# Attention scores over 160 key columns in column order, slipped between long products, and probabilities of two heads transposed together

## The chip, the cores and the metric

One core of a Trainium2 chip runs the whole kernel. The time is the device time of one execution in microseconds (us); lower is better. The engines in the profile are PE (TensorE, matrix products), PEld (TensorE loading the stationary operand of a product), DVE (VectorE), ACT (ScalarE), POOL (GpSimd) and SP (SyncE, which issues most transfers).

## The reference

An encoder of two layers on 256 tokens of width 1024. The tokens are a grid of 4 rows by 64 columns.

```
for l in range(DEPTH):                                   # 2
    x = x + 0.5 * swiglu(rms_norm(x), gate, up, down)    # width 2816
    z = rms_norm(x) @ w_in                               # 1024 -> 4352
    qa, ka, va, qs, ks, vs, zg = split(z)
    o_na = neighbourhood_attention(norm(qa), norm(ka), va, rpb)      # 8 heads of 64
    o_sw = sliding_window_gqa(norm(qs), norm(ks), vs, t5_bias, sink) # 8 heads, 2 kv heads
    g = sigmoid(zg + b_gate)
    x = x + (g_A * (o_na @ P_A) + g_B * (o_sw @ P_B)) @ w_out
    x = x + 0.5 * swiglu(rms_norm(x), gate2, up2, down2)
```

In the neighbourhood attention a query at grid column c sees all 4 rows of a window of 16 columns around c, clamped at the borders, with a bias per head from a table of relative rows and columns. All other scores are masked. In the sliding-window attention a query sees the keys up to 128 tokens away, with a bias by relative position (the same for both layers) and a sink term in the sum. Token s stands at row s // 64 and column s % 64.

## The kernel before

The 256 tokens are two tiles (t = 0, 1) of 128 partitions. All products are made in three parts: each operand is split into a high part and the rest (`wh` by ScalarE, `wl` by VectorE, in `split_to`, lines 184 and 185), and `three` (lines 170 to 172) adds xh wh, xh wl and xl wh into one PSUM bank. Such a product has 512 columns and is called a long product here.

TensorE's order is written by hand: Python emits its instructions in the order in which the chip runs them. `tick` advances a counter `now` by one for each three long products, and what was put aside with `defer(lag, ...)` is emitted when the counter reaches its time; `need` emits it earlier. The order on the other engines is made by a scheduler, which prefers what stands under `high_priority` (`urgent` below).

A layer is ffn, mix, ffn. `mix` makes its projections in the order of the string `ORDER` (Q, K: sliding-window queries and keys; q, k, v: those of the grid; g: gates; aN: the next of the 16 heads comes due N ticks later), so attention runs between the long products of the projections. `attend` handles a head in three steps:

- `front`: four score products (two token tiles, high and low part of the keys, line 568) into a bank of the tag "sc" (two buffers); VectorE adds the bias and takes the maximum (line 571), ScalarE the exponentials with their sums (line 574) and for the sliding window the sink `es` (line 578), VectorE the reciprocal, GpSimd scales the probabilities `S` (line 581).
- `turn`, `P_LAG` = 10 ticks later: TensorE transposes the four 128 x 128 blocks of `S` into the bank "pt" (one buffer, line 589), and `split_to` makes `ph` and `pl`.
- `back`, `V_LAG` = 7.5 ticks later: four products with the values (line 603) into one half of the bank "po" (one buffer, one tile for two heads); ScalarE copies the one part of it (`o`, line 607), VectorE adds the other (line 608); after the odd head `o` is split into `oA` or `oB`.

`MORE` adds ticks to the lag of single heads. `gates` (lines 655, 656) is an addition on VectorE and a tanh on ScalarE. `relative` fills a vector of 511 biases per head on GpSimd (line 484, 18 pieces) and stores it in device memory (`vec_d`); `sw_bias` loads 128 shifted rows of it per head. `na_bias` loads a head's part of the table in two transfers and GpSimd adds the mask of the columns (line 675). `S` is one of `LAG` = 3 buffers.

Of the kernel before, what the change touches and what calls it, by code (L numbers as in the profile page):

```python
# [21 lines left out]
P = 128  # L22
# [14 lines left out]
HB = NRR * NRC  # L37
T2W = 5 * NRC + GW
# [20 lines left out]
def hybrid_encoder(ctx, tc, x, w_gu1, w_d1, w_in, b_gate, qk_gain, rpb, sink, t5,  # L59
# [36 lines left out]
    qkg = const.tile([P, L, 4], F32, name="qkg")  # L96
    mask = const.tile([P, GW], F32, name="mask")
    snk = const.tile([P, L * NH], F32, name="snk")
# [13 lines left out]

    pad(const, "pad_c", 416)
    blank = ring.tile([P, 2, 512], F32R, name="blank", tag="wl", bufs=RING)
# [49 lines left out]
    def tick(cost):  # L164
        now[0] += cost
        while later and later[0][0] <= now[0]:
            later.pop(0)[3]()

    def three(ps, xh, xl, wh, wl, first, last):
        nc.tensor.matmul(ps, xh, wh, start=first, stop=False)  # L170
        nc.tensor.matmul(ps, xh, wl, start=False, stop=False)  # L171
        nc.tensor.matmul(ps, xl, wh, start=False, stop=last)  # L172

# [297 lines left out]

    vec_d = dram.tile([NH, 511], F32, name="vec_d")

    def relative():
        vec = act.tile([P, 512], F32, name="vec", tag="xg", bufs=2)[:NH, :511]
        table = small.tile([NH, 32], F32, name="table", tag="table", bufs=1)
        with tc.issue_after(rstd_done[0].ins):
            nc.gpsimd.dma_start(vec, c_band)
            nc.gpsimd.dma_start(table, t5)
        for a, n, b, step in _runs(_t5_constants()[0]):  # L480
            src = table[:, b:b + 1].to_broadcast([NH, n]) if step == 0 else table[:, min(b, b + step * (n - 1)):][:, :n]
            if step < 0:
                src = flipped(src)
            nc.gpsimd.tensor_tensor(vec[:, a:a + n], vec[:, a:a + n], src, ALU.add)
        nc.gpsimd.dma_start(vec_d, vec)

    def mix(l, n, after):
        with tc.tile_pool(name="mix", bufs=1) as mp:
# [51 lines left out]

            def attend(name, ins, qT, kh, kl, kidx, bias_of, vcol, ready, oT, sink_l=None):
                oh, ol = oT
                po = [None, None]
                with tc.issue_after(rstd_done[0].ins):
                    bias = [bias_of(0), bias_of(1)]
# [8 lines left out]
                def front(h):  # L554
# [3 lines left out]
                    b = bias.pop(0)  # L558
                    least = FMAX
# [3 lines left out]
                    S_ = mp.tile([P, T, S], F32, name="S", tag="S", bufs=LAG)  # L563
                    mx = small.tile([P, T], F32, name="mx", tag="mx")
                    sm = small.tile([P, T], F32, name="sm", tag="sm")
                    for t in range(T):
                        for i, k in enumerate((kh, kl)):
                            nc.tensor.matmul(ps[:, t, :], qT[:, h, t * P:(t + 1) * P], k[:, kidx(h), :],  # L568
                                             start=i == 0, stop=i == 1)
                    for t in range(T):  # L570
                        nc.vector.tensor_tensor_reduce(S_[:, t, :], ps[:, t, :], b(t), -1.0, least,  # L571
                                                       ALU.add, ALU.min, mx[:, t:t + 1])
                    for t in range(T):
                        nc.scalar.activation(S_[:, t, :], S_[:, t, :], AF.Exp, bias=mx[:, t:t + 1], scale=-1.0,  # L574
                                             accum_out=sm[:, t:t + 1])
# [4 lines left out]
                    nc.vector.reciprocal(sm, sm)  # L580
                    nc.gpsimd.tensor_tensor(S_, S_, sm.unsqueeze(2).to_broadcast([P, T, S]), ALU.mult)  # L581
                    defer(P_LAG + MORE.get((name, h), 0), (name, h, 0), lambda: turn(h, S_))

                @urgent
                def turn(h, S_):
                    tp = ps_acc.tile([P, T, T, P], F32, name="pt", tag="pt")
                    for t in range(T):
                        for kt in range(T):
                            nc.tensor.transpose(tp[:, kt, t, :], S_[:, t, kt * P:(kt + 1) * P], ident)  # L589
                    ph = mp.tile([P, T, T, P], F32R, name="ph", tag="ph", bufs=2)  # L590
                    pl = mp.tile([P, T, T, P], F32R, name="pl", tag="pl", bufs=2)
                    split_to(ph, pl, tp)
                    defer(V_LAG, (name, h, 1), lambda: back(h, ph, pl))

# [63 lines left out]
            def sw_bias(h):  # L658
                b = mp.tile([P, 384], F32, name="t5b", tag="t5b", bufs=2)
                nc.sync.dma_start(b, bass.AP(tensor=vec_d.tensor, offset=vec_d.offset + h * 511, ap=[[1, P], [1, 384]]))  # L660
                return lambda t: b[:, P - t * P:P - t * P + S]

            def na_bias(h):
                t2 = mp.tile([P, T2W], F32, name="t2", tag="t2", bufs=2)
                for r in range(2):
                    nc.sync.dma_start(
                        t2[r * GW:(r + 1) * GW],
                        bass.AP(tensor=rpb.tensor,
                                offset=rpb.offset + (l * NH + h) * HB + (4 + r) * NRC + 15 - (GW - 1),
                                ap=[[1, GW], [1, T2W]]))  # L670
                b = mp.tile([P, T, ROWS, GW], F32, name="b", tag="b", bufs=2)
                base = t2[:, :]
                src = bass.AP(tensor=base.tensor, offset=base.offset + 2 * NRC,
                              ap=[base.ap[0], [-2 * NRC, T], [NRC, ROWS], [1, GW]])
                nc.gpsimd.tensor_tensor(b, src, mask[:, None, None, :].to_broadcast([P, T, ROWS, GW]), ALU.add)
                return lambda t: b[:, t].rearrange("p r c -> p (r c)")
# [3 lines left out]
            na = attend("na", ("q0", "q1", "k0", "k1"), qT, *kT, lambda h: h, na_bias,  # L680
                        lambda kt, h: va[:, kt, h, :], lambda: "v1" in done, oA)
            step = {
# [10 lines left out]
            for token in ORDER.split():  # L693
# [7 lines left out]
            need(*[("front", True, h) for h in range(NH)])  # L701

            def branch(br, acc, t, pieces, ks):
# [88 lines left out]
def _window_constant():  # L792
    q = np.arange(GW)[:, None]
    k = np.arange(GW)[None, :]
    start = np.clip(q - 8, 0, GW - 16)
    m = np.where((k >= start) & (k < start + 16), 0.0, NEG).astype(np.float32)
    return np.ascontiguousarray(np.concatenate([m, m], 0)[::-1])

# [46 lines left out]
```

## Time and profile before

| | |
|---|---|
| time, median of 3 runs | 1076.77 us (1076.62 to 1077.98) |
| profiled execution: time, span | 1076.94 us, 1075.2 us |
| granted clock of TensorE | 0.999 |
| busy: PE, DVE, ACT, POOL | 1068.2, 875.8, 671.5, 116.7 us |
| VectorE in line 185 (`wl` from `raw`) | 336 of 1219 ns each |
| ScalarE in line 184 (`wh` from `raw`) | 336 of 1045 ns each |
| transfers | 212.63 MB, 198 GB/s |

The span runs from the first to the last instruction of the execution, and the time contains some microseconds around it. In a row of the timeline stand the start in us, the duration in us, the engine, the line, the operation and what it writes and reads, with partitions x elements; "xN" joins N of them, and brackets hold the idle time before it and what ended it. In a row of the groups stand count, then busy time in us and mean ns of one, then the idle time before them and what released it.

### The profile page before, as it was taken

The page shows a single profiled execution, that of the slowest core. Times are in us where ns is not written, and L with a number is a line of the kernel's source. Part 1 is how long each engine was busy: PE and PEld are TensorE (multiplying, and loading weights), DVE is VectorE, ACT ScalarE, POOL GpSimd, SP SyncE. Part 2 cuts the span into 40 slices and gives each one's busy share as a digit, 9 for nine tenths or more (in the row PEclk, how much of TensorE's full clock was granted, in tenths as well). Part 3 has the DMA queues.
Part 4 walks back from the last instruction along what each step waited for, and adds up shares of the span by engine and source line. Part 5 has one row for each costly group of instructions (what it writes and reads, how often), then busy time and mean ns, then how long its engine had stood idle before and what let it go on. Part 6 is the DMA issues. An engine that isn't in the chain of part 4 may idle for free.

```text
span 1075.2 us, 14749 instructions
## 1 busy us (share of the span) xinstructions
PE 1068.2 (99%) x5125; PEld 890.3 (83%) x5125; DVE 875.8 (81%) x1337; ACT 671.5 (62%) x1014; POOL 116.7 (11%) x118
## 2 busy tenths in 40 slices
PE   8999999999999999999999999999999999999998
PEld 6888888888888888888888888888888888888887
DVE  6678799889886768869977887988898867778696
ACT  6566654788764556565565665557877646566552
POOL 1000120243520000000000000003534000000000
PEclk9999999999999999999999999999999999999999
DMA  7767656765654667756657765657666554776652
GB/s 247 227 214 237 215 190 191 228 194 155 192 188 137 198 199 246 242 168 191 214 162 238 227 213 185 199 153 247 177 195 185 176 175 160 237 231 203 188 196 89
DMA packets 98827, 212.63 MB, mean 198 GB/s; under 512 B 7568, under 2 KB 13744, under 8 KB 98752
## 3 DMA queue, kind: packets, MB, share of 16 engines
q1 hardware_dynamic: 98560, 211.60, 62.3%
q8 instruction: 40, 0.66, 0.2%
q14 instruction: 35, 0.29, 0.1%
q0 software_dynamic: 192, 0.08, 0.1%
HBM read 210.59 MB, written 1.06 MB: 197 GB/s over the span
## 4 chain that ended last, share of the span: by engine, by line
PE 97%; DMA 1%; ACT 1%; DVE 0%; issue 0%; SPq 0%; ACTq 0%
PE g L170 22%; PE g L172 22%; PE g L171 22%; PE acc L170 5%; PE acc L172 5%; PE acc L171 5%; PE tp L320 2%; PE sc L568 1%; PE po L603 1%; PE tp L170 1%; PE tp L171 1%; PE tp L172 1%; PE pt L589 1%; PE tp L201 1%; PE br L170 1%; PE br L171 1%
## 5 line engine op out<-in xcount | busy, mean ns | idle before, releaser
L185 DVE TENSOR_TENSOR wl<-raw,wh 128x1024 fp32r<-128x1024 f32 x336 | 405.7, 1219 | 65.5 <-ACT wh L184 61.8
L184 ACT ACTIVATE wh<-raw 128x1024 fp32r<-128x1024 f32 x336 | 346.7, 1045 | 117.3 <-DMA raw<-in_w_gu 51.4
L170 PE MATMUL g<-wh,xh 128*128 128x512 f32 (+1 forms) x976 | 383.1, 393 | 0.5 <-DVE hh L444 0.5
L172 PE MATMUL g<-wh,xl 128*128 128x512 f32 (+1 forms) x976 | 377.8, 387 | 0.0
L171 PE MATMUL g<-wl,xh 128*128 128x512 f32 (+1 forms) x976 | 377.5, 387 | 0.0
L172 PEld LDWEIGHTS g<-wh,xl 128*128 128x128 f32 x976 | 183.4, 188 | 39.1 <-DVE xl L185 1.5
L170 PEld LDWEIGHTS g<-wh,xh 128*128 128x128 f32 x976 | 183.6, 188 | 33.8 <-DVE hh L444 1.1
L171 PEld LDWEIGHTS g<-wl,xh 128*128 128x128 f32 x976 | 183.7, 188 | 33.4 <-DVE wl L185 0.6
L443 ACT ACTIVATE sg<-g,rs_y 128x256 f32<-128x256 f32 x88 | 41.1, 467 | 89.7 <-PE g L172 77.3
L444 DVE SCALAR_TENSOR_TENSOR hh<-g,rs_y,sg 128x256 f32<-128x256 f32 x88 | 42.3, 481 | 53.0 <-ACT sg L443 53.0
L170 PE MATMUL acc<-wh,hi 128*128 128x512 f32 x180 | 71.2, 395 | 0.0
L171 PE MATMUL acc<-wl,hi 128*128 128x512 f32 x180 | 70.2, 390 | 0.0
L172 PE MATMUL acc<-wh,lo 128*128 128x512 f32 x180 | 70.1, 390 | 0.0
L176 POOL TENSOR_TENSOR rs_y<-ms,mhalf 128x1 f32<-128x1 f32 x12 | 8.1, 678 | 556.5 <-DVE ms L222 548.0
L352 DVE TENSOR_TENSOR u<-raw 128x512 f32<-128x512 f32 x64 | 41.7, 686 | 20.9 <-DMA raw<-in_w_d 20.8
L184 ACT ACTIVATE corner<-raw 128x512 fp32r<-128x512 f32 x32 | 20.1, 629 | 40.4 <-DMA raw<-in_w_d 22.4
L581 POOL TENSOR_TENSOR S<-S,sm 128x512 f32<-128x512 f32 x32 | 37.2, 1161 | 65.6 <-DVE sm L580 38.3
L172 PEld LDWEIGHTS acc<-wh,lo 128*128 128x128 f32 x180 | 33.8, 188 | 7.2
L171 PEld LDWEIGHTS acc<-wl,hi 128*128 128x128 f32 x180 | 33.8, 188 | 6.7
L170 PEld LDWEIGHTS acc<-wh,hi 128*128 128x128 f32 x180 | 33.8, 188 | 6.7
L184 ACT ACTIVATE wh<-v 128x1024 fp32r<-128x1024 f32 x20 | 21.2, 1062 | 28.9 <-DVE v L352 24.5
L574 ACT ACTIVATE S<-S,mx 128x256 f32<-128x256 f32 x64 | 31.9, 499 | 8.0 <-DVE mx L571 7.9
(189 smaller groups left out, 1522.0 us busy)
## 6 DMA issues: line engine op xcount, KB each, us to landing
raw<-in_w_gu SPq DMA_DIRECT2D x176, 512.0 KB, 4.5
raw<-in_w_d SPq DMA_DIRECT2D x100, 512.0 KB, 4.2
raw<-in_w_in SPq DMA_DIRECT2D x64, 512.0 KB, 4.7
raw<-in_w_out SPq DMA_DIRECT2D x16, 512.0 KB, 3.6
bb<-in_b_gate SPq DMA_DIRECT2D x16, 256.0 KB, 3.6
raw<-in_w_bsw SPq DMA_DIRECT2D x8, 512.0 KB, 3.9
raw<-in_w_bna SPq DMA_DIRECT2D x8, 512.0 KB, 3.5
raw<-in_w_d SPq DMA_DIRECT2D x12, 256.0 KB, 2.7
```

The lines of the kernel that those rows point to most:

```text
L170: nc.tensor.matmul(ps, xh, wh, start=first, stop=False)
L171: nc.tensor.matmul(ps, xh, wl, start=False, stop=False)
L172: nc.tensor.matmul(ps, xl, wh, start=False, stop=last)
L184: linked("act", lambda: nc.scalar.activation(hi, src, AF.Copy))
L185: linked("dve", lambda: nc.vector.tensor_tensor(lo, src, hi.bitcast(F32), ALU.subtract))
L201: nc.tensor.transpose(tp[:, i, :], xs[t][:, k * P:(k + 1) * P], ident)
L320: nc.tensor.transpose(tp[:, SLOT[t][i], :], hh[:, t, i * P:(i + 1) * P], ident)
L352: sub = lambda to, x, y: nc.vector.tensor_tensor(to, x, y, ALU.subtract)
L443: linked("act", lambda: nc.scalar.activation(sg, ps[:, :FC], AF.Silu, scale=rstd[t]))
L444: linked("dve", lambda: nc.vector.scalar_tensor_tensor(pair[0][:, t], ps[:, FC:], rstd[t], sg, op0=ALU.mult, op1=ALU.mult))
L574: nc.scalar.activation(S_[:, t, :], S_[:, t, :], AF.Exp, bias=mx[:, t:t + 1], scale=-1.0, accum_out=sm[:, t:t + 1])
L581: nc.gpsimd.tensor_tensor(S_, S_, sm.unsqueeze(2).to_broadcast([P, T, S]), ALU.mult)
```

## The change

- The host permutes the tokens to column order (token = column * 4 + row) and the result back. A tile of 128 tokens is then 32 columns, and its windows lie in 40 columns: 160 keys instead of 256 (`NKEY`, `keys_of`). The grid scores, maxima, exponentials and scalings are 160 wide. The probabilities lie in five lasting tiles `R0` to `R4`, whose 96 other columns GpSimd clears at the start of each layer's mix.
- The first of a grid head's four scores is emitted in its place, the other three one by one behind the next long products, through the list `between` that `three` empties. The rest of `front` is `soften`, emitted with the last score.
- `turn` takes two heads, when the odd one is due. The first head's transposes go into a bank of the tag "po", the second's into "pt". `back` then runs for both heads, one directly after the other.
- `relative` stores four copies of the table, one for each grid row, each reordered by a ScalarE copy (`one`, 508 wide) and stored by a GpSimd transfer of its own. `na_bias` loads a head's table in one transfer instead of two and builds the bias in two halves.
- `LAG` is 5 instead of 3.

```diff
-LAG = 3
+LAG = 5
...
     def three(ps, xh, xl, wh, wl, first, last):
-        nc.tensor.matmul(ps, xh, wh, start=first, stop=False)
-        nc.tensor.matmul(ps, xh, wl, start=False, stop=False)
-        nc.tensor.matmul(ps, xl, wh, start=False, stop=last)
+        for x, w in ((xh, wh), (xh, wl), (xl, wh)):
+            nc.tensor.matmul(ps, x, w, start=first and x is xh and w is wh, stop=last and x is xl)
+            if between:
+                between.pop(0)()
...
-        nc.gpsimd.dma_start(vec_d, vec)
+        table_d = act.tile([P, 512], F32, name="one", tag="xg", bufs=2)
+        for r in range(ROWS):
+            one = table_d[32 * r:32 * r + NH, :DIAG * ROWS]
+            src = bass.AP(tensor=vec.tensor, offset=vec.offset + GW * r, ap=[vec.ap[0], [1, DIAG], [GW, ROWS]])
+            nc.scalar.activation(one.rearrange("p (u k) -> p u k", k=ROWS), src, AF.Copy)
+            nc.gpsimd.dma_start(vec_d[:, r, :], one)
...
+                    def score(t, i, k):
+                        nc.tensor.matmul(ps[:, t, :n], qT[:, h, t * P:(t + 1) * P], k[:, kidx(h), keys_of(t)],
+                                         start=i == 0, stop=i == 1)
+                    rest = lambda begun=now[0]: soften(h, b, ps, S_, mx, sm, least, sk, begun)
...
+                    if rows:
+                        scores[1:] = [urgent(fn) for fn in scores[1:]]
+                        scores[0]()
+                        while between:
+                            between.pop(0)()
+                        between.extend(scores[1:-1])
+                        between.append(lambda: (scores[-1](), rest()))
...
-                    defer(P_LAG + MORE.get((name, h), 0), (name, h, 0), lambda: turn(h, S_))
+                    held.append((h, S_))
+                    if h % 2:
+                        pair_, held[:] = list(held), []
+                        defer(P_LAG + MORE.get((name, h), 0) + begun - now[0], (name, h, 0), lambda: turn(pair_))
...
-                def turn(h, S_):
-                    tp = ps_acc.tile([P, T, T, P], F32, name="pt", tag="pt")
-                    for t in range(T):
-                        for kt in range(T):
-                            nc.tensor.transpose(tp[:, kt, t, :], S_[:, t, kt * P:(kt + 1) * P], ident)
...
-                    defer(V_LAG, (name, h, 1), lambda: back(h, ph, pl))
+                def turn(heads):
+                    tps = [ps_acc.tile([P, T, T, P], F32, name="pt", tag=tag) for tag in ("po", "pt")]
+                    for (_, S_), tp in zip(heads, tps):
+                        for t in range(T):
+                            for kt in range(T):
+                                nc.tensor.transpose(tp[:, kt, t, :], S_[:, t, kt * P:(kt + 1) * P], ident)
...
+                    defer(V_LAG, (name, heads[1][0], 1), lambda: [back(*r) for r in ready_])
...
+            rows = [mp.tile([P, T, S], F32, name=f"R{i}", tag=f"R{i}") for i in range(LAG)]
+            for r in rows:
+                nc.gpsimd.memset(r[:, 0, NKEY:], 0.0)
+                nc.gpsimd.memset(r[:, 1, :S - NKEY], 0.0)
...
-    x_in[:, HEAD:] = a["x"].reshape(S, D)
+    x_in[:, HEAD:] = a["x"].reshape(ROWS, GW, D).transpose(1, 0, 2).reshape(S, D)
```

How the rows of work move shows at three places. In these rows `g`, `po`, `pt` and `sc` are the bank written, and the rest names what is read.

TensorE before, first layer, sliding window: the last product of head 3 and then the transposes of head 5.

```order
L603 MATMUL po<-pl,sv 128x256
L170 MATMUL g<-wh,xh_1793 128x512
L171 MATMUL g<-wl,xh_1793 128x512
L172 MATMUL g<-wh,xl_1794 128x512
L170 MATMUL g<-wh,xh_1793 128x512
L171 MATMUL g<-wl,xh_1793 128x512
L172 MATMUL g<-wh,xl_1794 128x512
L589 MATMUL pt<-ident,S 128x128 x4
```

The bank "pt" of these transposes is not that of the products ahead of them. TensorE after, first layer, the last sliding-window turn (heads 6 and 7), behind the products of heads 4 and 5.

```order
L648 MATMUL po<-ph,sv 128x256
L648 MATMUL po<-pl,sv 128x256
L177 MATMUL g<-wh,xh_1745 128x512
L177 MATMUL g<-wl,xh_1745 128x512
L177 MATMUL g<-wh,xl_1746 128x512
L177 MATMUL g<-wh,xh_1745 128x512
L177 MATMUL g<-wl,xh_1745 128x512
L177 MATMUL g<-wh,xl_1746 128x512
L631 MATMUL pt<-ident,S 128x128 x8
```

The two rows of `po` end a group of eight, the same six long products follow, and the turn is one of eight transposes, the first four of them into the bank of `po`. Next TensorE before at a grid head's scores.

```order
L172 MATMUL g<-wh,xl_1794 128x512
L568 MATMUL sc<-kh,qT 128x256
L568 MATMUL sc<-kl,qT 128x256
L568 MATMUL sc<-kh,qT 128x256
L568 MATMUL sc<-kl,qT 128x256
L170 MATMUL g<-wh,xh_1793 128x512
```

The four scores stand together. TensorE after, at the first grid head.

```order
L587 MATMUL sc<-kh,qT 128x160
L177 MATMUL g<-wh,xh_1745 128x512
L587 MATMUL sc<-kl,qT 128x160
L177 MATMUL g<-wl,xh_1745 128x512
L587 MATMUL sc<-kh,qT 128x160
L177 MATMUL g<-wh,xl_1746 128x512
L587 MATMUL sc<-kl,qT 128x160
```

A long product stands between each two of them. Last VectorE before, at the products of the sliding-window heads 6 and 7 (`sm` is the sum of a head's exponentials).

```order
L185 TENSOR_TENSOR wl<-raw,wh 128x1024
L580 RECIPROCAL sm<-sm 128x2
L608 TENSOR_TENSOR o<-o,po 64x256
L185 TENSOR_TENSOR wl<-raw,wh 128x1024 x2
L185 TENSOR_TENSOR pl<-pt,ph 128x512
L608 TENSOR_TENSOR o<-o,po 64x256
```

Each head's addition `o` stands between other work. VectorE after, at the products of the sliding-window heads 2 and 3, behind which the turn of heads 4 and 5 comes.

```order
L705 SCALAR_TENSOR_TENSOR gate_1829<-g,rs_y,bb 128x512
L608 ISA S,mx<-sc,t5b,nsnk 128x256
L608 ISA mx 128x1
L608 ISA S,mx<-sc,t5b,nsnk 128x256
L608 ISA mx 128x1
L192 TENSOR_TENSOR wl<-raw,wh 128x1024
L616 TENSOR_TENSOR sm<-sm,es 128x2
L653 TENSOR_TENSOR o<-o,po 64x256
L617 RECIPROCAL sm<-sm 128x2
L653 TENSOR_TENSOR o<-o,po 64x256
```

The additions of both heads of a pair now stand one behind the other, behind a head's maxima (line 608) and a `wl`; the transposes of the next pair use their bank.

More of the change, by code (lines that the diff above doesn't have):

```diff
@@ L570, in front @@
-                    for t in range(T):
-                        nc.vector.tensor_tensor_reduce(S_[:, t, :], ps[:, t, :], b(t), -1.0, least,
+                    def score(t, i, k):
+                        nc.tensor.matmul(ps[:, t, :n], qT[:, h, t * P:(t + 1) * P], k[:, kidx(h), keys_of(t)],
+                                         start=i == 0, stop=i == 1)
+                    rest = lambda begun=now[0]: soften(h, b, ps, S_, mx, sm, least, sk, begun)
+                    scores = [lambda t=t, i=i, k=k: score(t, i, k) for t in range(T) for i, k in enumerate((kh, kl))]
@@ new lines, in front @@
+                    if rows:
[5 more added lines that the diff above has]
+                        between.append(lambda: (scores[-1](), rest()))
+                    else:
+                        for fn in scores:
+                            fn()
+                        rest()
+                @urgent
@@ L572, in front, with soften @@
+                def soften(h, b, ps, S_, mx, sm, least, sk, begun):
+                    live = [S_[:, t, keys_of(t)] for t in range(T)]
+                    for t in range(T):
+                        nc.vector.tensor_tensor_reduce(live[t], ps[:, t, :n], b(t), -1.0, least,
                                                        ALU.add, ALU.min, mx[:, t:t + 1])
                     for t in range(T):
-                        nc.scalar.activation(S_[:, t, :], S_[:, t, :], AF.Exp, bias=mx[:, t:t + 1], scale=-1.0,
+                        nc.scalar.activation(live[t], live[t], AF.Exp, bias=mx[:, t:t + 1], scale=-1.0,
@@ L680, in mix @@
             na = attend("na", ("q0", "q1", "k0", "k1"), qT, *kT, lambda h: h, na_bias,
-                        lambda kt, h: va[:, kt, h, :], lambda: "v1" in done, oA)
+                        lambda kt, h: va[:, kt, h, :], lambda: "v1" in done, oA, rows=rows)
             step = {
@@ L701, in mix @@
             need(*[("front", True, h) for h in range(NH)])
+            while between:
+                between.pop(0)()
             def branch(br, acc, t, pieces, ks):
```

73 lines of the change are left out of this document (41 added, 32 removed).

## Prediction

> **What bounds the kernel now.** I read the page first: busy shares, the clock by slices, the chain that ended last.
>
> ```profile
> span 1075.2 us, 14749 instructions
> PE 1068.2 (99%) x5125; PEld 890.3 (83%) x5125; DVE 875.8 (81%) x1337; ACT 671.5 (62%) x1014; POOL 116.7 (11%) x118
> PEclk9999999999999999999999999999999999999999
> PE 97%; DMA 1%; ACT 1%; DVE 0%; issue 0%; SPq 0%; ACTq 0%
> ```
>
> The chain is TensorE for 97% of the span, at full clock. The stretch that the change touches (224 to 330 us, the attention of one layer) was read by windows, for us, PE, PEld, DVE, ACT, POOL:
>
> ```profile
> 224.00:330.00 106.00, 106.00 (x580) 90.29 (x579) 92.00 (x193) 80.64 (x170) 37.84 (x29) 1.00 0.61 182
> ```
>
> TensorE has no idle time there, so whatever shortens or delays its row of work by 1 us moves the end by 1 us; other engines count only where TensorE waits for them. Next the timeline of TensorE around one turn (start, duration, line, operation). Durations overlap, since matmuls are pipelined; the price of one is the step from its start to the next start.
>
> ```profile
> 266.66 0.28 PE L603 MATMUL po<-ph,sv 128*128 128x256 f32 x1
> 266.77 0.28 PE L603 MATMUL po<-pl,sv 128*128 128x256 f32 x1
> ...
> 267.13 0.40 PE L170 MATMUL g<-wh,xh 128*128 128x512 f32 x1
> ...
> 268.30 0.39 PE L172 MATMUL g<-wh,xl 128*128 128x512 f32 x1
> 268.53 0.60 PE L589 MATMUL pt<-ident,S 128*128 128x128 f32 x4
> 268.88 0.48 PE L170 MATMUL g<-wh,xh 128*128 128x512 f32 x1
> 269.19 0.40 PE L171 MATMUL g<-wl,xh 128*128 128x512 f32 x1
> ...
> 269.66 0.28 PE L568 MATMUL sc<-kh,qT 128*128 128x256 f32 x1
> ...
> 270.02 0.28 PE L568 MATMUL sc<-kl,qT 128*128 128x256 f32 x1
> 270.14 0.40 PE L170 MATMUL g<-wh,xh 128*128 128x512 f32 x1
> 270.38 0.39 PE L171 MATMUL g<-wl,xh 128*128 128x512 f32 x1
> ```
>
> Prices: a long product (512 columns) 0.23 (six from 267.13 to 268.53 make 1.40); a 256-wide score or po product 0.12 (four from 269.66 to 270.14 make 0.48); the first long product behind such a group 0.24 (270.14 to 270.38).
>
> **The change part by part.** *Narrower scores.* 64 of TensorE's 5128 matmuls go from 256 to 160 columns, each now with a long product on both sides. No row has such a pattern. By width alone one would take 0.23 x 160/512 = 0.072. But each matmul also loads 128 columns of its own, and the nearest row for a matmul shorter than its successor's load is the end of a group of 128-wide transposes:
>
> ```profile
> 209.12 0.19 PEld L170 LDWEIGHTS g<-wh,xh 128*128 128x128 f32 x1
> 209.15 0.47 PE L170 MATMUL g<-wh,xh 128*128 128x512 f32 x1
> 209.23 0.19 PEld L171 LDWEIGHTS g<-wl,xh 128*128 128x128 f32 x1
> 209.46 0.40 PE L171 MATMUL g<-wl,xh 128*128 128x512 f32 x1
> ```
>
> The next load starts when the matmul ahead enters the array, and 209.12 to 209.23 is one load: 0.11. So a 160-wide score should cost 0.11, the load of the long product behind it, and not 0.072: 64 x (0.12 - 0.11) = 0.6 us gained; with the load hidden 64 x (0.12 - 0.072) = 3.1. I take 0.6, since 0.11 is read from a short matmul ahead of a long one, the same neighbours, and keep 3.1 as the end. The lower end is no gain.
>
> By the Trainium skill, page "TensorE: Matmul & The Clock Gate", section "LDWEIGHTS (loading the stationary operand)", a load takes about its columns over 1.2 ns, 107 ns for 128, whatever the contraction; that speaks against the narrowing, and the trace's 0.11 agrees. The same page's section "Back-to-back issue gap" gives N/2.4 + 2.5 ns, 69 ns for 160 columns, by which the gain would be 3.3 us; for 256 columns it gives 109 ns where this trace has 120, so the trace decides.
>
> *Four groups where one was.* Before, the four scores of a head stand together; after, each stands alone, so 48 more long products follow a short one. At 0.01 each (0.24 against 0.23) this is 0.5 us lost; ends 0 and 1.0. The 8 po products of two heads together make 16 fewer exits of that kind: -0.2.
>
> *Joined transposes.* Does a group of eight cost less than two of four? The nearest group of eight of the same width:
>
> ```profile
> 38.05 1.03 PE L320 MATMUL tp<-ident,hh 128*128 128x128 f32 x8
> 38.84 0.48 PE L170 MATMUL g<-wh,xh 128*128 128x512 f32 x1
> 39.16 0.39 PE L171 MATMUL g<-wl,xh 128*128 128x512 f32 x1
> ```
>
> Start to the second long product, less that one long product: eight cost 39.16 - 38.05 - 0.23 = 0.88, four 269.19 - 268.53 - 0.23 = 0.43. Twice four is 0.86: nothing gained.
>
> *The wait that comes with joining.* Before, every turn wrote bank "pt". Now the first head's four transposes write bank "po", which has one buffer and holds the products of the pair before until ScalarE's copy and VectorE's add (o) of both heads have read it. TensorE takes its row in order, so at that point it stops, with all long products queued behind it. How long after the first po product is a head's o done?
>
> ```profile
> 240.56 0.28 PE L603 MATMUL po<-ph,sv 128*128 128x256 f32 x1
> 241.23 0.38 ACT L607 ACTIVATE o<-po 64x256 f32<-64x256 f32 x1 [1.13 <-PE po L603]
> 241.64 0.41 DVE L608 TENSOR_TENSOR o<-o,po 64x256 f32<-64x256 f32 x1 [0.91 <-ACT o L607]
> ...
> 268.17 0.38 ACT L607 ACTIVATE o<-po 64x256 f32<-64x256 f32 x1
> ...
> 269.11 1.21 DVE L185 TENSOR_TENSOR wl<-raw,wh 128x1024 fp32r<-128x1024 f32 x1
> 270.25 0.41 DVE L608 TENSOR_TENSOR o<-o,po 64x256 f32<-64x256 f32 x1
> ```
>
> With both engines free, 242.05 - 240.56 = 1.49. The head whose products start at 266.66 needed 270.66 - 266.66 = 4.0: ScalarE finished a wh first, and VectorE a gate and two wl. For a pair the two o's alternate, ScalarE 0.38, VectorE 0.41 with 0.04 of hand-over each: 0.87 more, so 2.36 at best. By the written order TensorE reaches the turn after 8 po and six long products, 8 x 0.12 + 6 x 0.23 = 2.33, at three turns per layer: sliding-window heads 4 and 5, 6 and 7, and grid heads 6 and 7. Elsewhere 9 or 12 long products and up to four scores or eight transposes stand between (3.1 and more). The groups of the stretch give what is queued ahead of the o's (line, engine, operation, count | busy, mean ns | idle before):
>
> ```profile
> L185 DVE TENSOR_TENSOR wl<-raw,wh 128x1024 fp32r<-128x1024 f32 x30 | 38.0, 1273 | 6.4 <-ACT wh L184 6.4
> L184 ACT ACTIVATE wh<-raw 128x1024 fp32r<-128x1024 f32 x29 | 30.4, 1054 | 6.8 <-PE g L172 5.6 <-PE br L172 1.1
> L574 ACT ACTIVATE S<-S,mx 128x256 f32<-128x256 f32 x32 | 15.9, 499 | 4.0 <-DVE mx L571 4.0
> L655 DVE SCALAR_TENSOR_TENSOR gate<-g,rs_y,bb 128x512 f32<-128x512 f32 x8 | 5.9, 741 | 0.3 <-PE g L172 0.3
> L578 ACT ACTIVATE es<-mx,snk 128x2 f32<-128x2 f32 x8 | 2.3, 282 | 0.0
> ```
>
> Times from the moment at which TensorE wants the turn (first po at -2.33):
> - Heads 4, 5. ScalarE has first exp, wh, second exp, es ahead of its o's; wh becomes possible at -2.5 and ends at -1.46, the exp at -0.95, es at -0.67, the first copy at -0.29. VectorE's wl, which needs that wh, runs from -1.43 to -0.2, then sm, o to 0.35; copy to 0.77; second o to 1.2. Wait 1.2.
> - Heads 6, 7. The scores of the first grid head stand directly ahead of the po products; their reductions and exps run before and between the o's: the second o ends at 0.4. Wait 0.4.
> - Grid heads 6, 7. A gate (-2.84 to -2.1) and two wl, the second waiting for a wh that ends at -1.8, hold VectorE until 0.3; o, copy, o end at 1.5. Wait 1.5.
>
> The other turns end their walks 0.3 to 1.1 before TensorE comes. Both layers have the same order: 2 x (1.2 + 0.4 + 1.5) = 6.2 us. Ends: 0, if VectorE runs about a wl earlier than walked; and 2 x 3 x (4.0 + 0.87 - 2.33) = 15 if every tight turn is as late as the 4.0 above. I take the walk, since it orders the very rows. A wait lets both engines catch up, so the turn after it isn't late for it.
>
> *Table copies, queues.* Rows of ScalarE and GpSimd around the table:
>
> ```profile
> 140.41 0.60 ACT L184 ACTIVATE hi<-tp 128x512 fp32r<-128x512 f32 x1 [0.17 <-PE tp L320]
> 142.65 1.06 ACT L184 ACTIVATE wh<-v 128x1024 fp32r<-128x1024 f32 x1 [1.64 <-DVE v L352]
> 149.75 0.63 ACT L184 ACTIVATE corner<-raw 128x512 fp32r<-128x512 f32 x1 [2.68 <-DMA raw<-in_w_d]
> ...
> 132.09 9.24 POOL L484 TENSOR_TENSOR vec<-vec,table 8x165 f32<-8x165 f32 x18 [1.56 <-DMA vec<-in_c_band]
> 190.40 0.57 POOL L176 TENSOR_TENSOR rs_y<-ms,mhalf 128x1 f32<-128x1 f32 x1 [48.24 <-DVE ms L222]
> ```
>
> Four 508-wide copies stand behind hi, wait for the vector until 141.4 (132.09 + 9.24) and take about 0.55 each (hi, 512 wide, 0.60): until 143.6, so wh starts 1.0 late and ScalarE regains it in its 2.68 idle before 149.75. Nothing, with 1.0 as the upper end. GpSimd's three more table DMAs stand in its 48 us of idle; its 20 memsets and twice as many bias builds of half the work lie in its idle time (68 us of the 106 above); SP loses 16 DMAs. No turn waits longer for GpSimd's scaling by the order, since a pair's turn stands later behind its first head's scaling than before and its second head keeps its lag: nothing; if a pair's turn did wait, it would appear under rival two.
>
> The sum against the profiled execution (span 1075.2, 1.7 around it, 1076.9): -0.6 + 0.5 - 0.2 + 6.2 = +5.9, 1082.8. That execution is 0.2 above the median of the runs: 1082.7 forecast.
>
> **The rivals.** One: the waits as walked, but the load behind a score is hidden (0.072 a score): 2.4 us less, 1080.3. For it: in the rows of long products the loads are hidden; against it: 209.12 to 209.23. A reordering that pulls the load ahead, named by the Trainium skill, same page, section "LDWEIGHTS (loading the stationary operand)", would do this; here every load starts with or after the matmul before it.
>
> Two: more waits, each tight turn as late as the 4.0 of the row, 6 x 2.54 = 15, or two more turns per layer becoming late by about 1.3: 1088 to 1091. For it: the looser turns have as little as 0.3 in hand.
>
> Three, the other side: no wait. It decides at 2.33 against 2.36: where ScalarE and VectorE take the o's promptly, the bank is free as TensorE comes, and 1082.7 - 6.2 = 1076.5 is left, the same as before. For it: VectorE is 81% busy on the page, so it has spare time to run ahead of its queue; against it: in this stretch it is 92.0 of 106 busy, and one wl costs 1.27.
>
> Four: no wait and the load hidden: 1076.5 - 2.4 = 1074.1, faster.
>
> **How the numbers follow.** Forecast 0.56 (own range 1080.5 to 1085.5), rival one 0.15, two 0.08, three 0.13, four 0.08. The likeliest is 1082.7. The range takes in rival three and one and leaves out four and two: 1075.8 to 1087.4. A measurement tells about 0.2%, 2.2 us, from no change: faster is four less its tail above 1074.6 and rival three's below (0.08), same is three (0.14), slower the rest (0.78).
>
> **What the changed profile would show.** The scores: steps of 0.11 from each 160-wide score to the long product behind it (0.07 would prove rival one). The waits: idle time of TensorE ahead of the turns for heads 4 and 5, 6 and 7 of both kinds put down to VectorE's o, some 6 us in all, and TensorE's share of the chain lower by as much; without such rows rival three stands. ScalarE's copies: no idle of TensorE near 150. I would be wrong most of all if VectorE's queue stands ahead of where my walk puts it.

## The result

The changed kernel takes 1116.51 us (median of 4 runs, 1113.78 to 1118.25) against 1077.25 us (4 runs): 1.0362 times as long, interval 1.0349 to 1.0374. The forecast was 1082.7, with a range up to 1087.4. The direction was right and the size was not: 39 us were lost where 5.9 were forecast.

The page of the changed kernel, the same four lines as before:

```profile
span 1115.5 us, 14756 instructions
PE 1080.7 (97%) x5125; PEld 898.0 (81%) x5125; DVE 870.3 (78%) x1337; ACT 674.0 (60%) x1018; POOL 112.9 (10%) x157
PEclk9999999998999999999999999999999999999999
PE 81%; DVE 10%; ACT 3%; issue 3%; DMA 3%; POOL 0%; ACTq 0%; DVEq 0%; POOLq 0%
```

TensorE's share of the chain fell from 97% to 81%, VectorE's rose from 0 to 10%, and one slice of the clock is below full. The view of the waits names the place (us in total, times, longest):

```profile
PE po L648 <- DVE o L653: 27.8, 16, 2.3
```

TensorE does not wait at the turns. It waits inside the group of eight value products, once for each of the 16 pairs of heads. The timeline of TensorE at the first pair:

```profile
249.91 0.28 PE L648 MATMUL po<-ph,sv 128*128 128x256 f32 x1
...
250.26 0.28 PE L648 MATMUL po<-pl,sv 128*128 128x256 f32 x1
252.86 0.54 PE L648 MATMUL po<-ph,sv 128*128 128x256 f32 x1 [2.32 <-DVE o L653]
...
253.84 0.63 PE L177 MATMUL g<-wh,xh 128*128 128x512 f32 x1
254.26 0.63 PE L177 MATMUL g<-wl,xh 128*128 128x512 f32 x1
...
256.51 0.48 PE L177 MATMUL g<-wh,xh 128*128 128x512 f32 x1
256.83 0.40 PE L177 MATMUL g<-wl,xh 128*128 128x512 f32 x1
```

Four products of the first head run from 249.91. The second head's first product starts at 252.86, 2.60 after the product ahead of it, where 0.12 is its step: 2.48 lost. Over the 16 pairs these excess steps add up to 30.4 us (1.08 to 2.48 each). What ScalarE and VectorE did meanwhile:

```profile
249.92 1.21 DVE L192 TENSOR_TENSOR wl<-raw,wh 128x1024 fp32r<-128x1024 f32 x1
...
250.38 0.49 ACT L611 ACTIVATE S<-S,mx 128x256 f32<-128x256 f32 x1
...
250.88 0.49 ACT L611 ACTIVATE S<-S,mx 128x256 f32<-128x256 f32 x1
...
251.13 1.21 DVE L192 TENSOR_TENSOR wl<-raw,wh 128x1024 fp32r<-128x1024 f32 x1
...
251.67 0.38 ACT L652 ACTIVATE o<-po 64x256 f32<-64x256 f32 x1
...
252.40 0.40 DVE L653 TENSOR_TENSOR o<-o,po 64x256 f32<-64x256 f32 x1
```

Exponentials stand ahead of the first head's copy and two `wl` ahead of its addition, and as soon as that addition ends (252.80) the second head's products start (252.86). The two heads share one bank (one tile, `po`), and in this kernel a product waits until the other engines have done their reads of what was written there before it, although it writes the other half.

After the stop a long product takes 0.42 instead of 0.23 (253.84 to 254.26). Three windows of 3.41 us around it; behind the length stand the busy time of PE, PEld, DVE, ACT and POOL, then the granted clock, the busy share of the DMA engines and GB/s:

```profile
249.52:252.94 3.41, 1.10 (x8) 0.81 (x6) 3.36 (x11) 2.50 (x7) 0.37 (x1) 1.00 0.83 245
252.94:256.35 3.41, 3.41 (x13) 3.02 (x14) 1.33 (x3) 1.78 (x4) 1.67 (x2) 0.50 0.87 290
256.35:259.76 3.41, 3.41 (x23) 2.99 (x22) 2.94 (x5) 2.35 (x5) 0.00 (x0) 1.00 0.27 49
```

The clock is halved for exactly one such window, 1.7 us lost. There are five of them in the execution: 8.5 us. The rest of the loss lies far away, at 181 to 190 us, in three waits of 0.68, 1.00 and 0.35, 2.0 in all (below). 30.4 + 8.5 + 2.0 = 40.9 against a difference of spans of 40.3.

### The profile page after: what moved, and what is told of

It reads as the page before. It is cut to its first block, busy times and chain, and to the rows that moved or that the text cites. A ratio compares the mean times of both kernels' runs of the same rounds, so it can differ in the third digit from the quotient of the medians.

```text
span 1115.5 us, 14756 instructions
## 1 busy us (share of the span) xinstructions
PE 1080.7 (97%) x5125; PEld 898.0 (81%) x5125; DVE 870.3 (78%) x1337; ACT 674.0 (60%) x1018; POOL 112.9 (10%) x157
## 4 chain that ended last, share of the span: by engine, by line
PE 81%; DVE 10%; ACT 3%; issue 3%; DMA 3%; POOL 0%; ACTq 0%; DVEq 0%; POOLq 0%
PE g L177 58%; PE acc L177 10%; DVE wl L192 4%; DMA raw<-in_w_d 2%; PE br L177 2%; PE tp L177 2%; ACT wh L191 2%; PE tp L327 2%; PE po L648 1%; PE pt L631 1%; PE g L244 1%; PE tp L208 1%; PE sc L587 1%; DVE v L359 1%; DVE corner L192 1%
## 5 line engine op out<-in xcount | busy, mean ns | idle before, releaser
L177 PEld LDWEIGHTS g<-wl,xh 128*128 128x128 f32 x976 | 184.7, 189 | 34.6 <-DVE wl L192 0.6
L192 DVE TENSOR_TENSOR lo<-a,hi 128x896 fp32r<-128x896 f32 x32 | 33.8, 1086 | 0.6 <-ACT hi L191 0.6
L191 ACT ACTIVATE hi<-a 128x896 fp32r<-128x896 f32 x32 | 29.1, 942 | 7.9 <-DVE a L340 7.8
```

What stands on the lines that cost most here:

```text
L177: nc.tensor.matmul(ps, x, w, start=first and x is xh and w is wh, stop=last and x is xl)
L191: linked("act", lambda: nc.scalar.activation(hi, src, AF.Copy))
L192: linked("dve", lambda: nc.vector.tensor_tensor(lo, src, hi.bitcast(F32), ALU.subtract))
```

## The experiments

**Is it the joining?** `pairs_before` is the kernel before with only the joining (and five S buffers); `single` is the changed kernel with one head at a time. The main lines of the edit of `single` (`turn` and `back` then handle one head, as before):

```diff
-                    held.append((h, S_))
-                    if h % 2:
-                        pair_, held[:] = list(held), []
-                        defer(P_LAG + MORE.get((name, h), 0) + begun - now[0], (name, h, 0), lambda: turn(pair_))
+                    defer(P_LAG + MORE.get((name, h), 0) + begun - now[0], (name, h, 0), lambda: turn(h, S_))
...
```

> The kernel before with the joining alone: transposes of two heads together in the banks po and pt, the backs of both heads one after the other, five S buffers; old layout, four scores together, no table copies. Theory (bank): 16 stops of TensorE on VectorE's o, about 30 us, and 4 to 6 stretches of half clock, 7 to 10 us: 1112 to 1118. Rival (rest of the change): below 1095.

> The changed kernel with turn and back for one head at a time as before; column layout, 160-wide scores between long products, ScalarE's table copies and five S buffers stay. Theory (bank): the joining carries 38.9 of the loss, the table copies 2.0 and the scores 0: 1077.5 to 1080. Rival (rest of the change): layout, scores or copies carry a good part: 1085 or more.

Measured: `pairs_before` 1123.82 (ratio 1.0424, 1.0407 to 1.0442), `single` 1078.24 (1.0009, 1.0000 to 1.0018). The joining alone makes the whole loss and more, and `pairs_before` lies above its expected range of 1112 to 1118: its 16 stops come to 34.6 us by the steps, and nine windows, in eight stretches, have half clock. The view of its waits:

```profile
PE po L611 <- DVE o L616: 32.0, 16, 3.1
```

All the rest of the change costs about 1 us, the table copies below included.

**Is it the shared bank?** `banks` writes the second head's products into the other bank; `emit8` keeps one bank, but the program writes all eight products down ahead of the reads, so TensorE's row is the same word for word.

```diff
# banks
-                    if h % 2 == 0:
-                        po[0] = ps_acc.tile([P, 2, T, P], F32, name="po", tag="po")
+                    po[0] = ps_acc.tile([P, 2, T, P], F32, name="po", tag=("po", "pt")[h % 2])
# emit8, in back, now called once for both heads
+                    for h, ph, pl in heads:
+                        for kt in range(T):
+                            for i, p in enumerate((ph, pl)):
+                                nc.tensor.matmul(po[0][:, h % 2], vcol(kt, h), p[:, kt], start=kt + i == 0,
+                                                 stop=kt + i == 2)
+                    for h, ph, pl in heads:
...
+                        nc.scalar.activation(o[a:a + DH], ov[b:b + DH], AF.Copy)
+                        nc.vector.tensor_tensor(o[a:a + DH], o[a:a + DH], ov[a:a + DH], ALU.add)
```

> The changed kernel with the second head's value products in the bank of the tag pt, and the first head's in po. Theory (bank): no stop inside a pair, no half clock, 1116.5 - 38.9 = 1077.6; the second head's transposes come 0.4 us later than the first's, so the walked waits at the six tight turns come to about 4 us: 1078 to 1082. Rival (late engines): 1100 or more, with waits of the turns' transposes on VectorE's o.

> The changed kernel with one edit: all eight value products of a pair are written down ahead of the copy and the addition of both heads, so that TensorE's row stays the same and only its waits differ. Theory (bank): the second head's products stand in the bank that ScalarE and VectorE are reading for the first head, and TensorE stops 16 times, 30.4 us, which also brings 5 stretches of 3.4 us at half clock (8.5 us). Then both go, 38.9 us, and what may come is a wait at the three tight turns of a layer: my walk gave 6.2 us for the six, and reading starts 0.5 us later for each. Expected 1078 to 1087, best guess 1084. Rival (late engines): VectorE is behind whatever the bank, and the same wait only moves to the next turn: 1100 or more.

`banks` took 1082.98 (1.0055, 1.0040 to 1.0070), 0.98 above its expected interval; no stop in a pair, no half clock. What is left above `single` are waits at the three turns that the prediction had walked: 2.1 us per layer, 4.2 in all, one of them in the timeline of TensorE:

```profile
265.33 1.09 PE L631 MATMUL pt<-ident,S 128*128 128x128 f32 x8 [0.26 <-DVE o L653]
```

`emit8` took 1108.84 (1.0298, 1.0277 to 1.0320), and that is the rival's number. The stops left the pairs and came back at the turns, with three windows at half clock. Timeline of `emit8` at the first of them:

```profile
253.00 0.38 ACT L653 ACTIVATE o<-po 64x256 f32<-64x256 f32 x1
...
253.73 0.40 DVE L654 TENSOR_TENSOR o<-o,po 64x256 f32<-64x256 f32 x1
253.78 1.05 ACT L191 ACTIVATE wh<-raw 128x1024 fp32r<-128x1024 f32 x1
...
254.73 1.25 ACT L543 ACTIVATE kh<-tp,qkg 128x512 fp32r<-128x512 f32 x2
...
256.01 0.38 ACT L653 ACTIVATE o<-po 64x256 f32<-64x256 f32 x1
...
257.44 0.42 DVE L654 TENSOR_TENSOR o<-o,po 64x256 f32<-64x256 f32 x1
...
258.01 1.41 PE L631 MATMUL pt<-ident,S 128*128 128x128 f32 x8 [2.03 <-DVE o L654]
```

The second head's copy stands behind a short copy, a `wh` and two `kh`, 2.6 us after the first head's copy, and TensorE waits for the addition behind it. My reading: written first or not, copy, addition, copy, addition take turns in one bank, and the scheduler fills the pauses with long work. `emit8_copies_first` tests it and writes both copies ahead of both additions.

```diff
+                    for add in (False, True):
+                        for h, ph, pl in heads:
...
+                            if add:
+                                nc.vector.tensor_tensor(o[a:a + DH], o[a:a + DH], ov[a:a + DH], ALU.add)
+                            else:
+                                nc.scalar.activation(o[a:a + DH], ov[b:b + DH], AF.Copy)
```

> As emit8 (1108.84), and the two copies of a pair are written down ahead of the two additions. Theory (alternation): emit8 lost at the turns because copy, addition, copy, addition follow one another in one bank and the scheduler filled the second copy's waiting time with weights and keys, up to 3 us of other work ahead of it; with both copies first they stand next to each other in ScalarE's row, and what is left are waits near my walk, 6 to 10 us for all turns: 1116.5 - 38.9 + 8, 1082 to 1090. Rival (late VectorE): the additions are late whatever the order: 1100 or more.

1089.81 (1.0119, 1.0105 to 1.0133), the top of the expected range. The waits at turns on VectorE's addition, first in `emit8` and then here:

```profile
PE pt L631 <- DVE o L654: 19.9, 14, 3.1
```

```profile
PE pt L631 <- DVE o L656: 6.3, 6, 1.3
```

All stops of the two layers' attention together come to 10.7 us by the steps, 7.3 at the three walked turns and 3.4 at the products that use `oA`, and no window has half clock. So the order of four short instructions in two queues is worth 19 us, with TensorE's row unchanged; some 5 of them are the three windows of `emit8`'s profiled execution. No run separates the bank from the tile: `banks` gives the second head another bank and another tile at once.

**A dose.** `apart1` puts three long products between the two heads' products.

```diff
-                    defer(V_LAG, (name, heads[1][0], 1), lambda: [back(*r) for r in ready_])
+                    for q, r in enumerate(ready_):
+                        defer(V_LAG + 1 * q, (name, r[0], 1), lambda r=r: back(*r))
```

> The changed kernel with the second head's products three long products (0.69 us) behind the first head's. Theory (bank, and the clock by idle share): each of the 16 stops is 0.69 shorter, 11 us, and since none is above 1.8 us no stretch has half clock, 8.5 us; the turns that follow come 0.69 later, so they wait at most 1 us more at the six tight ones: 1097 to 1102. Rival (clock by any stop over 1 us): the half clock stays, 1105 or more.

1110.05 (1.0306, 1.0292 to 1.0320): outside the theory's range of 1097 to 1102 and in the rival's, 1105 or more. The stops in the pairs moved as expected: in this view they are 17.0 instead of 27.8 us, 0.67 less each. One window instead of five has half clock, where the theory had none; no stop here is above 1.94, but parts of two stops, 0.77 and 1.37 us, fall into the window before it (266.01 to 269.43). So the rival's reason, that any stop over 1 us brings half clock, fails although its number fits. What I had too small is the turn, which comes 0.69 earlier after the second head's products:

```profile
PE po L649 <- DVE o L654: 17.0, 16, 1.8
PE pt L631 <- DVE o L654: 4.2, 6, 1.5
```

By the steps the stops after the pairs come to 8.4 us, 5.0 at the turns and 3.4 at the products that use `oA`; in the changed kernel they are 0. The time put between the two heads was taken from the time between head and turn.

**The 2 us at 181 to 190.** All kernels with the table copies on ScalarE show these waits. In the changed kernel ScalarE's copies and what follows, and the first of the waits 35 us later:

```profile
140.26 4.63 ACT L496 ACTIVATE one<-vec 8x508 f32<-8x508 f32 x4
144.91 1.06 ACT L191 ACTIVATE wh<-v 128x1024 fp32r<-128x1024 f32 x1
...
181.38 0.50 PE L177 MATMUL acc<-wl,hi 128*128 128x512 f32 x1 [0.52 <-DVE wl L192]
```

A copy takes 1.16 and not the 0.55 of the prediction. `single_gps` puts the copies on GpSimd:

```diff
-            nc.scalar.activation(one.rearrange("p (u k) -> p u k", k=ROWS), src, AF.Copy)
+            nc.gpsimd.tensor_copy(one.rearrange("p (u k) -> p u k", k=ROWS), src)
```

> One head at a time as in the run before it, and the four table copies on GpSimd instead of ScalarE. Theory (copies): ScalarE's 4.6 us of copies at 140 us delay the low parts of the weights on a VectorE that is 95% busy there, and TensorE pays 2.05 us between 181 and 190 us; with the copies on GpSimd that goes: 1078.24 - 2.05 = 1076.2, and the three waits of TensorE there with it. Rival (other): the waits there have another cause, such as the first transfers of the next stage: 1078.2, the same three waits.

1079.06 (1.0021, 1.0012 to 1.0030) where 1076.2 was expected, no better than `single`. The waits at 181 to 190 went, but a new one of 2.19 us came at 144.7, with a window at half clock behind it, and VectorE is slower beside GpSimd's copies:

```profile
141.15 6.04 POOL L496 COPY one<-vec 8x508 f32<-8x508 f32 x4
...
143.17 3.09 DVE L359 TENSOR_TENSOR u<-raw 128x512 f32<-128x512 f32 x2
```

The same two `u` take 1.29 in `single`, where no copies run on GpSimd. `single_dma` and `banks_dma` wrote the tables with 32 transfers in pieces of 4 bytes:

> One head at a time, and no engine copies the table: 32 small GpSimd transfers write the four reordered tables straight from the vector. single_gps showed that copies on GpSimd stretch VectorE's two u from 1.29 to 3.09 us, so they only moved the loss. Theory (copies): with no copy on any engine VectorE is not late at 146 us and the three waits between 181 and 190 us (2.05 in single) go: 1078.24 - 2.05 = 1076.2. Rival (other): they stay, 1078.2.

> As banks (1082.98), with the tables written by transfers as in single_dma. Theory (sum of parts): the 2.5 us of waits between 181 and 190 us go and the 4.2 us of waits at the turns stay: 1080.5. Rival (the parts hide each other): a TensorE that isn't late at 190 us reaches the turns earlier and waits more there: 1083.

1418.59 and 1422.17. The transfers land one after another, about 11 us each, and hold a buffer that the next normalisation needs; in `single_dma` VectorE waits once for it:

```profile
DVE xg L215 <- DMA vec_d<-vec: 310.4, 1, 310.4
```

These runs say nothing on the copies, and neither expected number was near. The last pair does that part of the change alone, on the kernel before; its table is read by nothing. In `before_copies_flat` the source is `vec[:, r:r + 508]`, read in a row into other numbers, and the rest is the same.

```diff
...
+        table_d = act.tile([P, 512], F32, name="one", tag="xg", bufs=2)
+        for r in range(4):
+            one = table_d[32 * r:32 * r + NH, :508]
+            src = bass.AP(tensor=vec.tensor, offset=vec.offset + GW * r, ap=[vec.ap[0], [1, 127], [GW, 4]])
+            nc.scalar.activation(one.rearrange("p (u k) -> p u k", k=4), src, AF.Copy)
+            nc.gpsimd.dma_start(one_d[:, r, :], one)
```

> The kernel before, plus the four 8 x 508 copies on ScalarE and their four transfers into a table that nothing reads. Theory (copies): each reads with a step of 64 elements and takes 1.16 us, wh from v starts 2 us late, VectorE waits 2 us for it and stays behind, TensorE pays 2 us at the end of the stage: 1077.0 + 2.0 = 1079.0, with three waits of TensorE between 181 and 190 us. Rival (other parts of the change): 1077.0, no waits there.

> As before_copies, with copies that read unit step (other numbers in the unread table). If the step makes the 1.16 us, each takes 0.55 to 0.6, wh starts at most 1 us late and VectorE 0.3: 1077.0 to 1077.4. If the 8 partitions or the count make it, each takes 1.16 again and the time is that of before_copies, 1079.0.

`before_copies` 1079.16 (1.0018, 1.0010 to 1.0027), `before_copies_flat` 1077.59 (1.0003, 0.9994 to 1.0012), both against 1077.06. Their timelines, the stepped copies first:

```profile
140.18 4.62 ACT L491 ACTIVATE one<-vec 8x508 f32<-8x508 f32 x4
...
145.92 1.23 DVE L185 TENSOR_TENSOR wl<-v,wh 128x1024 fp32r<-128x1024 f32 x1 [1.86 <-ACT wh L184]
```

```profile
141.85 2.58 ACT L491 ACTIVATE one<-vec 8x508 f32<-8x508 f32 x4 [1.02 <-POOL vec L485]
...
145.55 1.23 DVE L185 TENSOR_TENSOR wl<-v,wh 128x1024 fp32r<-128x1024 f32 x1 [1.34 <-ACT wh L184]
```

The copies alone cost 2.1 us, with waits of 0.66, 1.21 and 0.34 at 181 to 190. Reading with a step of 64 elements takes 1.16 a copy, reading in a row 0.65, and then the cost is not told from none. In the second kernel `wh` starts 1.8 late too, more than I expected, because its copies could not start before 141.85: they wait for GpSimd to fill the vector, which ended later in that execution (141.8 against 139.3). So the two kernels differ in more than the step. In the second one TensorE's steps show 0.70 and 0.35 at 184 and 188, about 1 us less in all; why 0.5 us at VectorE make 1 us at TensorE is not settled. The copies cost more than the 1.0 us by which `single` lies above the kernel before; whether the rest of the change gains the difference, no run shows.

**Do the scores pay to stand apart?** Timeline of TensorE and its loads in `single`, at one grid head:

```profile
301.84 0.23 PE L587 MATMUL sc<-kh,qT 128*128 128x160 f32 x1
301.84 0.19 PEld L177 LDWEIGHTS g<-wh,xh 128*128 128x128 f32 x1
301.91 0.43 PE L177 MATMUL g<-wh,xh 128*128 128x512 f32 x1
301.95 0.19 PEld L587 LDWEIGHTS sc<-kl,qT 128*128 128x128 f32 x1
302.18 0.23 PE L587 MATMUL sc<-kl,qT 128*128 128x160 f32 x1
```

A score takes 0.07 and the long product behind it 0.27 instead of 0.23: 0.34 for the two, 0.11 for the score. The two loads start 0.11 apart, as the prediction had read. The hidden-load rival asked for 0.07 in all; the prediction's sign for it, a step of 0.07 from score to long product, is met by these rows and proves nothing, since the long product then takes 0.04 more. `single_gps_grouped`, `single_dma_grouped` and `single_grouped` put the four together again:

```diff
-                    if rows:
-                        scores[1:] = [urgent(fn) for fn in scores[1:]]
...
+                    for fn in scores:
+                        fn()
+                    rest()
```

> As single_gps, with a grid head's four 160-wide scores together instead of between long products. In the trace of the changed kernel an isolated score costs 0.072 of its own and delays the next step by 0.045, 0.117 in all. Theory (load): inside a group each score is held up by the load of the next, 0.11, so grouping is worth 64 x 0.007, 0.5 us: 1075.7. Rival (stream): inside a group the loads are hidden and a score takes 0.072: 64 x 0.045, 2.9 us less, 1073.3.

> As single_dma, with a grid head's four 160-wide scores together. Steps read from the traces: isolated 0.073 + 0.042 = 0.115 each, together 0.113, 256 wide 0.119. Theory (load): 64 x 0.002, no difference to single_dma that shows: 1076.1, and 0.4 below the kernel before. Rival (stream): 3 us below single_dma.

> As single (1078.24), with a grid head's four 160-wide scores together. Theory (load): 64 x 0.002, the same as single to 0.3 us. Rival (stream): 3 us less, 1075.

1081.33, 1416.29 and 1078.91. The first two carry the disturbances above: 1081.33 is 2.3 us above `single_gps`, but four of its five executions have a mean clock of 0.998, like the profiled execution of `single_gps` with its window at half clock, and only three of the eleven of `single_gps` have it. The third is `single` (1078.24) within the scatter of both, 1.0015 (1.0007 to 1.0024) against the kernel before, where `single` has 1.0009 (1.0000 to 1.0018). The place of the scores makes no difference that shows, and the 3 us less of the stream rival are excluded. No version here beats the kernel before.

## Why the prediction was wrong, point by point

- **The step that failed: "By the written order TensorE reaches the turn after 8 po and six long products, 8 x 0.12 + 6 x 0.23 = 2.33".** The eight were priced as one group (the sum is 2.34, which changes nothing). I charged the shared bank "po" to its next user, the next pair's transposes, and not to the second half of the same pair. The sum had no term for a wait between the two heads of a pair. The rows that I quoted had the price: a head's o ends 1.49 to 4.0 after its first product, and its own four products cover 0.48. That is a stop of 1.0 to 3.5 for every pair, not for three turns per layer, 16 to 56 us for 16 pairs; measured were 1.08 to 2.48 each and 30.4 in all. The Trainium skill, page "PSUM — Partial Sum Buffer", section "PSUM bank collisions raise a hardware error", has the rule: guard by bank and quadrant, not by address. The 16 waits here agree with it: the second head writes other columns of the same bank and waits all the same. Whether the halves could be used at once on the chip was not tried.
- **"Wait 1.2 ... 0.4 ... 1.5", 6.2 us at the turns.** In the changed kernel these are 0, because the stop in the pair takes their place. So the direction came out right by luck: the only large loss that was forecast did not occur in this kernel. With the stop removed they are 4.2 us at the same turns in `banks` and 7.3 in `emit8_copies_first`: the mechanism was right and its sum of the right size, though the single waits were not (0.41, 0.98 and 0.69 in `banks` for the walked 1.2, 0.4 and 1.5). In `emit8_copies_first` the products that use `oA` wait another 3.4, a place that I had not walked.
- **No term for the clock.** 8.5 us in the profiled execution, five windows at half clock. The sum asked what TensorE waits for, and not what its own idle time then does to its clock.
- **"Table copies ... Nothing, with 1.0 as the upper end."** 2.1 us. Two errors: the copy's price came from an instruction that reads in a row (0.60, and such copies do take 0.65), and the cover, ScalarE's 2.68 of idle at 149.75, was that of the wrong engine. VectorE, which waits for that `wh`, is 58.8 us busy in the 62 before 192 us of the kernel before (the third busy time in its row of the windows) and has little room to catch up:

```profile
130.00:192.00 62.00, 62.00 (x282) 51.31 (x281) 58.80 (x78) 35.62 (x45) 10.87 (x21) 1.00 0.53 171
```

- **Scores, "a 160-wide score should cost 0.11".** Right: 0.11, and nothing won by narrowing that shows. The reordering named under rival one stands in the Trainium skill, page "TensorE: Matmul & The Clock Gate", in the section "Step-by-step: what each phase is for", not in the one that the prediction gives. No load in the traces of the kernel before and of `single` starts ahead of the matmul in front of it.
- **Joined transposes, "nothing gained".** Right as far as the rows show: eight took 0.79 to the next long product in the changed kernel as in the rows of before.
- **Rival two (more waits)** was nearest in kind, but its 1088 to 1091 still counted turns only. That half of the range which lay below 1082.7 rested on the other rivals, all of which assumed that the pair itself was free.

## What to carry to other kernels

When operations of one kind are joined into a larger group, look for everything that passes between the halves: in a shared bank the first half's readers stand between them, and the group's price is the readers' latency, queues and all. Ask of each wait of a full engine not only what stands behind it, but, for TensorE, whether its idle share lowers its own clock. And take the cover of a moved operation from the engine that waits for its result, at its business in that stage, not from the idle time of the engine that runs it.

## What the runs showed of the hardware that was not expected

Within one execution all changes of TensorE's clock lie on a grid of 3.41 us. In these runs a window at full clock was followed by one at half clock if TensorE was idle for more than about 1.9 us of it. Over the thirteen profiled executions without the 4-byte transfers (the kernel before among them) all 16 windows with 2.05 us or more of idle time between matmuls were followed by one of half clock, none of those at full clock with less than 1.90, and of those between 1.90 and 1.93 some were and some were not. The idle times are worked out from the starts of the matmuls, so they are good to about a tenth. One window stands outside this: in `pairs_before` a stop of 3.21 us ended 0.64 into a window that had half clock already (808.48 to 811.89), and the next one had half clock too. So that one stop cost two windows.

The grid is why two stops of 2.48 and 2.46 us in the changed kernel differ: the first lay in one window (249.5 to 252.9), the second was split 1.77 and 0.69 and brought no half clock. It also goes with the scatter of the changed kernel, 1113.8 to 1118.3 where the kernel before has 1076.6 to 1078.0: its fastest execution has a mean clock of 0.995, its slowest 0.992.

The Trainium skill, page "TensorE: Matmul & The Clock Gate", section "What's actually happening", gives a free-running window of 3413 ns, and the length agrees. It puts the return to half clock after an idle window, and here 56% of one sufficed.

A ScalarE copy of 8 x 508 that reads with a step of 64 elements takes 1.16 us, one that reads in a row 0.65. Beside GpSimd's copies of the same table two VectorE subtractions took 3.09 us instead of 1.29. GpSimd's transfers of 4-byte pieces, 512 elements each at most, landed one after another at about 11 us each.
